# Up projection of a two-layer decoder trunk: the 512-column and the 256-column products alternate row block by row block

## The chip, the core and the metric

The kernel runs on one core of one Trainium2 chip. The metric is the device time of one execution in microseconds (us). A core has TensorE for matrix products (PE in the profile, PEld where it loads weights), VectorE (DVE), ScalarE (ACT), GpSimd (POOL) and SyncE (SP), whose queue issues the transfers between device memory and on-chip memory. Products accumulate in PSUM, in banks of 128 partitions by 512 numbers of 32 bits.

## The reference, cut to what matters

Two layers, each with a mixing part (two groups of attention heads, left out here) and a multilayer perceptron with a squared ReLU. The change lies in `h @ w_up`. There are 256 tokens, the model width is 1024 and the hidden width 4096.

```python
for l in range(DEPTH):                      # DEPTH = 2
    ...
    x = x + _rms_norm(mix, g_post_mix[l])
    h = _rms_norm(x, g_pre_mlp[l])
    y = jnp.square(jax.nn.relu(h @ w_up[l])) @ w_down[l]
    x = x + _rms_norm(y, g_post_mlp[l])
```

All data is float32.

## The kernel before

**How a float32 product is made.** TensorE works on a reduced form of float32 here (type fp32r in the profile). Each operand is split into two parts: `hi` is the rounded value, written by ScalarE (`whi`, `aT`, `xT` with ACTIVATE), and `lo` is what is left, written by VectorE (`wlo` and so on with TENSOR_TENSOR). A product a·b is then hi·hi + hi·lo + lo·hi, summed in PSUM.

**Up projection** (function `up`, from line 1388). The hidden width is cut into 8 chunks of 512 (`fc`), the first of which has a function of its own (`up0`). For each of the chunks 1 to 7, `up` goes through 4 blocks `b` of 128 hidden columns. A block has one split weight of 128 x 1024 (`hi` and `lo`, eight row blocks `k` of 128 x 128) and one PSUM bank `ps` from the tag `s` (three banks). `xT[0]` and `xT[1]` are the hi and the lo part of the transposed activations, and `xT[2]` is the view that holds both beside each other: 2 x 256 = 512 columns for each `k`. So one product of `hi[:, k]` with the 512 columns gives hi·hi in the first half of the bank and hi·lo in the second, and one product of `lo[:, k]` with the 256 columns of `xT[0]` adds lo·hi to the second half. A block has eight of the one and eight of the other, and each loads its own 128 x 128 weights. Before, the eight products of 512 columns come first (lines 1394 to 1396) and then the eight of 256 columns (lines 1397 to 1399). ScalarE then takes the second half out of the bank, VectorE adds the first half to it (lines 1405 and 1406), and for each pair of blocks ReLU, square and the split into `aT` follow (lines 1407 to 1413).

Everything of this that TensorE does appears in the profile as `s<-xT,whi` (128x512) and `s<-xT,wlo` (128x256): 2 layers x 7 chunks x 4 blocks x 8 = 448 of each.

**Down projection.** After the 64 products of a chunk's up projection come the 48 of the down projection of the chunk before it (`down`), 512 columns each, into the four banks of the tags `x` and `acc`, which are held over all chunks.

**What sets the order.** The kernel is recorded first (class `Recorder`) and then ordered by a list scheduler with costs of its own. TensorE takes the ready product that was recorded first. All products into one PSUM bank keep their recorded order. ScalarE and VectorE take what is due first, where the due times are worked back from the planned order of TensorE's products. Each engine then runs its list in order. Weights come through three rings: 9 raw tiles that SyncE's queue fills, 7 `whi` and 7 `wlo` tiles; loads are recorded 12 weights ahead and splits one ahead, and the scheduler may pull them further forward. All recorded instructions are issued at line 392, so that the profile shows that line for all of them, and they are told apart by the names of their tiles.

Of the kernel before, what the change touches and what calls it, by code (L numbers as in the profile page):

```python
# [503 lines left out]
def trunk(nc, A, consts_in, out, sbp, pp):  # L504
    def tile(shape, dtype, name, tag=None, bufs=1):
        return nc.tile(sbp[(tag or name) not in OPERANDS], shape, dtype, name, tag, bufs)

    def psum(tag):
        return nc.tile(pp, [P, 512], F32, tag, tag, {"acc": 2, "x": 2, "s": 3, "o": 1}[tag], psum=True)

    def small(shape, name, bufs=2):
        return tile(shape, F32, name=name, tag=name, bufs=bufs)
# [50 lines left out]
    def weight(*key):  # L563
        return W.get(index[key])
# [210 lines left out]
    for l in range(DEPTH):  # L775
# [612 lines left out]
        def up(fc, then=None):  # L1388
            a = [tile([P, 4, S], F32R, name="aT", tag=f"act{j}", bufs=2) for j in range(2)]
            for b in range(4):  # L1390
                hi, lo = weight(l, "up", fc, b)

                ps = psum("s")
                for k in range(8):
                    nc.tensor.matmul(ps, hi[:, k, :], xT[2][:, k].rearrange("p j n -> p (j n)"), start=k == 0, stop=False,
                                     skip_group_check=True)
                for k in range(8):
                    nc.tensor.matmul(ps[:, S:], lo[:, k, :], xT[0][:, k, :], start=False, stop=k == 7,
                                     skip_group_check=True)
                if then is not None and b == 1:  # L1400
                    then()
                if b % 2 == 0:
                    h = tokt("h")
                d = h[:, (b % 2) * S:(b % 2) * S + S]
                nc.scalar.activation(d, ps[:, S:], AF.Copy)
                nc.vector.tensor_add(d, ps[:, :S], d)
                if b % 2:
                    rl = small([P, 512], "rl")
                    nc.scalar.activation(rl, h, AF.Relu)
                    nc.vector.tensor_mul(h, rl, rl)  # L1410
                    d = [y[:, b - 1:b + 1, :].rearrange("p b n -> p (b n)") for y in a]
                    nc.scalar.activation(d[0], rl, AF.Square)
                    nc.vector.tensor_sub(d[1], h, d[0].bitcast(F32))
            return a
# [42 lines left out]
        for fc in range(8):  # L1457
            if fc < 7:
                nxt = up(fc + 1, then)
                then = None  # L1460
# [83 lines left out]
```

## Time and profile before

| | |
|---|---|
| median of 3 timed runs | 626.17 us (625.88 to 626.36) |
| profiled execution, its own time | 626.18 us |
| profiled execution, span from the first to the last instruction | 624.4 us |
| TensorE matmul busy | 615.1 us, 99% of the span |
| weight loads busy | 517.5 us, 83% |
| VectorE busy | 481.0 us, 77% |
| ScalarE busy | 378.4 us, 61% |
| read from device memory | 114.00 MB, 184 GB/s over the span |
| granted TensorE clock, mean | 0.998 of full speed |

Rows of the profile's groups read: line, engine, operation, tile written <- tiles read, shape, count | busy us, mean ns of one | idle time ahead of them. Rows of a timeline read: start in us from the span's start, length in us, engine, line, operation, and how many instructions in a row were merged. A matmul's length is more than its turn on the engine: products are pipelined, and the time that one adds is seen from its start to the start of the next.

### The profile page before, as it was taken

The numbers are of one execution on the slowest core, as the hardware profiler recorded it, in microseconds if no ns is written. First come the engines' busy times: TensorE is split into PE (matmuls) and PEld (weight loads), VectorE is DVE, ScalarE is ACT, GpSimd is POOL, SyncE is SP. The second block draws the span as 40 slices with busy tenths as digits, with TensorE's granted clock in tenths as the row PEclk, the third lists the DMA queues.
The fourth block names the chain that finished last, engine by engine and source line by source line (L and its number), as shares of the span: only waits on it lengthen the run. The fifth ranks groups of instructions, "written<-read, shape, count | busy, mean of one in ns | idle before, by whom it ended". The sixth has DMA issues, their size and how long they took to land.

```text
span 624.4 us, 9952 instructions
## 1 busy us (share of the span) xinstructions
PE 615.1 (99%) x3572; PEld 517.5 (83%) x3572; DVE 481.0 (77%) x1077; ACT 378.4 (61%) x736; POOL 0.2 (0%) x4
## 2 busy tenths in 40 slices
PE   9999999999999999999999999999999999999995
PEld 6988986788888888888888989778888888888884
DVE  6878999989986557566698899997997666566544
ACT  7757777577665455555566657764776555455432
POOL 0000000000000000000000000000000000000000
PEclk9999999999999999999999999999999999999999
DMA  8987446218766556654346883422396566556001
GB/s 322 403 341 257 150 153 199 88 56 318 266 192 203 194 175 201 198 180 136 102 156 218 303 290 118 164 81 90 105 318 204 183 186 209 180 189 193 22 1 68
DMA packets 33601, 115.70 MB, mean 185 GB/s; under 512 B 3984, under 2 KB 4112, under 8 KB 33552
## 3 DMA queue, kind: packets, MB, share of 16 engines
q1 hardware_dynamic: 33552, 115.07, 55.2%
q8 instruction: 28, 0.46, 0.3%
q14 instruction: 21, 0.17, 0.1%
HBM read 114.00 MB, written 1.05 MB: 184 GB/s over the span
## 4 chain that ended last, share of the span: by engine, by line
PE 91%; DVE 4%; DMA 2%; ACT 1%; issue 1%; DVEq 0%; SPq 0%
PE s L392 34%; PE acc L392 28%; PE x L392 24%; PE o L392 6%; DVE pr L392 2%; DMA wraw<-in_w_in_dram 1%; DVE wlo L392 1%; DMA first<-in_first_dram 1%; ACT whi L392 1%; ACT rl L392 0%; DVE cum L392 0%; DVE prT L392 0%; DVE st L392 0%; DVE prX L392 0%; ACT xT L392 0%
## 5 line engine op out<-in xcount | busy, mean ns | idle before, releaser
L392 DVE TENSOR_TENSOR wlo<-wraw,whi 128x1024 fp32r<-128x1024 f32 (+1 forms) x188 | 224.9, 1202 | 86.3 <-ACT whi L392 85.7
L392 ACT ACTIVATE whi<-wraw 128x1024 fp32r<-128x1024 f32 (+1 forms) x188 | 195.5, 1044 | 134.0 <-PE acc L392 70.3
L392 PE MATMUL s<-xT,whi 128*128 128x512 f32 x448 | 112.0, 392 | 0.0
L392 PEld LDWEIGHTS s<-xT,whi 128*128 128x128 f32 x448 | 81.4, 189 | 15.2
L392 PE MATMUL acc<-whi,aT 128*128 128x512 f32 x256 | 88.6, 390 | 0.0
L392 PE MATMUL x<-whi,aT 128*128 128x512 f32 x256 | 88.4, 390 | 0.0
L392 PEld LDWEIGHTS s<-xT,wlo 128*128 128x128 f32 x448 | 61.1, 190 | 4.4
L392 PE MATMUL s<-xT,wlo 128*128 128x256 f32 x448 | 62.5, 282 | 0.0
L392 PEld LDWEIGHTS acc<-whi,aT 128*128 128x128 f32 x256 | 48.0, 188 | 9.9
L392 PEld LDWEIGHTS x<-whi,aT 128*128 128x128 f32 x256 | 48.1, 188 | 9.6
L392 ACT ACTIVATE pr<-pr,st 128x256 f32<-128x256 f32 (+1 forms) x96 | 42.9, 450 | 15.6 <-DVE st L392 14.3
L392 PE MATMUL x<-wlo,aT 128*128 128x512 f32 x128 | 50.0, 390 | 0.0
L392 PE MATMUL acc<-wlo,aT 128*128 128x512 f32 x128 | 49.9, 390 | 0.0
L392 PE MATMUL acc<-xT,whi 128*128 128x256 f32 x256 | 48.8, 286 | 0.0
L392 PEld LDWEIGHTS acc<-xT,whi 128*128 128x128 f32 x256 | 40.4, 190 | 2.2 <-issue 1.2
L392 PE MATMUL x<-whi,xT 128*128 128x512 f32 x112 | 36.8, 400 | 0.4 <-ACT xT L392 0.3
L392 PE MATMUL acc<-xT,wlo 128*128 128x256 f32 x128 | 36.4, 285 | 0.0
L392 PE MATMUL acc<-whi,xT 128*128 128x512 f32 (+1 forms) x128 | 36.0, 352 | 0.0
L392 ACT ACTIVATE rl<-h 128x512 f32<-128x512 f32 x28 | 17.6, 629 | 18.2 <-DVE h L392 18.2
L392 PEld LDWEIGHTS acc<-wlo,aT 128*128 128x128 f32 x128 | 24.0, 188 | 5.0
L392 PEld LDWEIGHTS x<-wlo,aT 128*128 128x128 f32 x128 | 24.1, 188 | 4.5
L392 ACT ACTIVATE rl<-x 128x512 f32<-128x512 f32 x24 | 14.7, 612 | 21.6 <-PE x L392 16.6
(231 smaller groups left out, 974.7 us busy)
## 6 DMA issues: line engine op xcount, KB each, us to landing
wraw<-in_w_up_dram SPq DMA_DIRECT2D x64, 512.0 KB, 3.8
wraw<-in_w_down_dram SPq DMA_DIRECT2D x64, 512.0 KB, 3.6
wraw<-in_w_in_dram SPq DMA_DIRECT2D x36, 512.0 KB, 4.7
wraw<-in_w_out_dram SPq DMA_DIRECT2D x16, 512.0 KB, 6.2
w<-in_cmp_w_k_dram SPq DMA_DIRECT2D x8, 512.0 KB, 5.5
w<-in_cmp_w_v_dram SPq DMA_DIRECT2D x8, 512.0 KB, 5.8
first<-in_first_dram SPq DMA_DIRECT2D x7, 384.0 KB, 6.3
wraw<-in_w_in_dram SPq DMA_DIRECT2D x8, 288.0 KB, 4.2
```

The costliest lines, as they stand in the source:

```text
L392: getattr(getattr(self.nc, op.engine), name)(*[real(v) for v in args], **{k: real(v) for k, v in kw.items()})
```

## The change

The second loop header goes, so that the product of 256 columns is recorded right after the product of 512 columns of the same row block `k`. Both loops had the same range. The number of products, their operands, the first (`start`) and the last (`stop`) of each bank stay as they are; only the order within each of the 56 blocks differs.

```diff
                 for k in range(8):
                     nc.tensor.matmul(ps, hi[:, k, :], xT[2][:, k].rearrange("p j n -> p (j n)"), start=k == 0, stop=False,
                                      skip_group_check=True)
-                for k in range(8):
                     nc.tensor.matmul(ps[:, S:], lo[:, k, :], xT[0][:, k, :], start=False, stop=k == 7,
                                      skip_group_check=True)
                 if then is not None and b == 1:
```

In the program that comes out, TensorE's list has the same products in the same order outside these blocks, and within them the two kinds by turns. The lists of ScalarE and VectorE, which the scheduler orders by due times, differ in some places from the first changed block on (a split of a weight changes places with a step of the activation, above all); SyncE's list of transfers is the same.

## The prediction

> **What bounds the kernel now.** I read the page first: the busy shares, the granted clock over the span, the chain that ended last, and the groups of the changed products.
>
> ```profile
> PE 615.1 (99%) x3572; PEld 517.5 (83%) x3572; DVE 481.0 (77%) x1077; ACT 378.4 (61%) x736; POOL 0.2 (0%) x4
> ...
> PEclk9999999999999999999999999999999999999999
> ...
> PE 91%; DVE 4%; DMA 2%; ACT 1%; issue 1%; DVEq 0%; SPq 0%
> ...
> L392 PE MATMUL s<-xT,whi 128*128 128x512 f32 x448 | 112.0, 392 | 0.0
> ...
> L392 PE MATMUL s<-xT,wlo 128*128 128x256 f32 x448 | 62.5, 282 | 0.0
> ```
>
> TensorE is busy through 99% of the span at its full clock, 91% of the chain is its own work, and the two groups that the change reorders never stood idle for anything (0.0 in the last column). So a stretch of the up projection costs what its products cost on TensorE, and a change there reaches the end undiminished, to gain or to lose. Next I read the chain in order of time, for the size of an up stage, and the windows over one stage.
>
> ```profile
> 166.93 11.15 PE s L392 x64
> ...
> 584.82 11.15 PE s L392 x64
> ```
>
> ```profile
> core 0: us, PE busy (x) PEld busy (x) DVE busy (x) ACT busy (x) POOL busy (x), PEclk, DMA share, GB/s
> 144.24:155.81 11.57, 11.57 (x68) 10.14 (x67) 11.15 (x16) 7.78 (x12) 0.00 (x0) 1.00 0.87 315
> 166.77:177.92 11.15, 11.15 (x66) 9.83 (x65) 10.68 (x15) 8.03 (x15) 0.00 (x0) 1.00 0.62 195
> 451.89:463.54 11.65, 11.65 (x70) 10.32 (x69) 11.61 (x16) 8.12 (x12) 0.00 (x0) 1.00 0.93 329
> ```
>
> These are the first and the last of 12 equal stages of 64 products: 11.15 us each, though VectorE's load and the transfers differ between stages. The first up stage of each layer also holds other products (11.57 and 11.65 us, the outer rows of the windows); I price its own 64 alike. So the changed part is 14 stages of 11.15 us, 156.1 us, a quarter of the span. A stage has 32 pairs of one 512 and one 256: **348.4 ns a pair** as it is now.
>
> Then TensorE's timeline of one stage, for what each kind costs by itself, and the view by tile for the lengths.
>
> ```profile
> 166.77 1.98 PE L392 MATMUL s<-xT,whi 128*128 128x512 f32 x8
> 168.58 1.12 PE L392 MATMUL s<-xT,wlo 128*128 128x256 f32 x8
> 169.54 2.00 PE L392 MATMUL s<-xT,whi 128*128 128x512 f32 x8
> 171.38 1.12 PE L392 MATMUL s<-xT,wlo 128*128 128x256 f32 x8
> 172.33 2.00 PE L392 MATMUL s<-xT,whi 128*128 128x512 f32 x8
> 174.17 1.11 PE L392 MATMUL s<-xT,wlo 128*128 128x256 f32 x8
> 175.12 2.00 PE L392 MATMUL s<-xT,whi 128*128 128x512 f32 x8
> 176.96 1.12 PE L392 MATMUL s<-xT,wlo 128*128 128x256 f32 x8
> 177.92 0.40 PE L392 MATMUL x<-whi,aT 128*128 128x512 f32 x1
> ```
>
> ```profile
> L392 PE MATMUL s<-xT,whi x448: 389/389/478, 144.2 to 594.6; 128*128 128x512 f32 x150
> L392 PE MATMUL s<-xT,wlo x448: 277/283/283, 146.1 to 595.7; 128*128 128x256 f32 x150
> ```
>
> From start to start, eight 256s take 168.58 to 169.54, 0.96 us: 120 ns each. Eight 512s take 1.81 us (226 each) where they follow other 512s (166.77 to 168.58), but 1.84 us (230 each) where they follow 256s (169.54 to 171.38). So going back from 256s to 512s is not free: the four blocks take 2.77, 2.79, 2.79 and 2.80 us, and the three dearer ones are those that follow 256s. Lengths are modelled, but they follow the step: 389 against 226 and 283 against 120 are both 163 more, so a step is the length less 163 ns, finer than the timeline's rounding to 10 ns.
>
> **The change, part by part.** Nothing is added or removed: TensorE runs the same 448 + 448 products with as many weight loads, in 448 alternating pairs, and its list outside the blocks is the same. So the sum has one term, the price of a pair by turns, and some side effects.
>
> *The pair.* No up stage alternates, so the price comes from the nearest rows: one spot where 512s stand singly among 256s, of the same type and with their own weights, and one where two 512s stand together.
>
> ```profile
> 359.47 0.40 PE L392 MATMUL acc<-xT,whi 128*128 128x256 f32 x2
> 359.71 0.40 PE L392 MATMUL x<-kx,qS 128*128 128x512 f32 x1
> 359.94 0.28 PE L392 MATMUL acc<-xT,wlo 128*128 128x256 f32 x1
> 360.06 0.40 PE L392 MATMUL x<-kx,qS 128*128 128x512 f32 x1
> 360.30 0.40 PE L392 MATMUL acc<-xT,whi 128*128 128x256 f32 x2
> 360.54 0.28 PE L392 MATMUL acc<-xT,wlo 128*128 128x256 f32 x1
> ```
>
> ```profile
> L392 PE MATMUL x<-kx,qS 128*128 128x512 f32 x2 | 0.8, 400 | 0.0
> ...
> L392 PE MATMUL acc<-xT,wlo 128*128 128x256 f32 x1 | 0.3, 281 | 0.0
> ```
>
> ```profile
> 63.18 0.28 PE L392 MATMUL acc<-xT,wlo 128*128 128x256 f32 x1
> 63.30 0.63 PE L392 MATMUL x<-kx,qS 128*128 128x512 f32 x2
> 63.77 0.39 PE L392 MATMUL acc<-xT,whi 128*128 128x256 f32 x2
> 64.00 0.28 PE L392 MATMUL acc<-xT,wlo 128*128 128x256 f32 x1
> ```
>
> The first and second of these fences are one spot (timeline, and groups in the window 359.70 to 360.29). From the first 512's start to 360.30 is 0.59 us for 512, 256, 512; with the next 256 (half of the 0.24 to 360.54) the two pairs take 0.71 us, **355 ns a pair**. The lengths agree: 400 less 163 is 237 for a 512 and 281 less 163 is 118 for the 256 between them, together 355. So a single 512 after a 256 costs some 11 ns more than in a run, and the 256 after it gives back only 2. In the third fence the pair of 512s takes 0.47 us, 235 each, and the two 256s after it 0.23, 115 each: there the give-back is larger. Bounds for a pair by turns:
>
> - low end 346: the 512 costs 232 (a first one after 256s; 0.23 at 359.71) and the 256 gets 114, its shortest (277 less 163 in the view by tile);
> - high end 361: 241 for the 512 (0.24 at 360.06, the later of the two, when the alternation had gone on longest) and a full 120 for the 256;
> - taken 355.5, the row's own mean over two pairs, which is the only one that alternates.
>
> At 355.5 a stage takes 32 x 355.5 = 11.38 us, 0.23 more than 11.15; 14 stages give **+3.2 us**. The low end gives 11.07 and -1.1 us, the high end 11.55 and +5.6 us.
>
> *The lo weights are needed sooner.* The first `wlo` product stood 8 x 226 = 1.81 us after the block began and will stand 0.23 after it, so VectorE's split must be done 1.6 us sooner. The shortest lead is at the first block of layer 0:
>
> ```profile
> 137.91 3.49 DVE L392 TENSOR_TENSOR wlo<-wraw,whi 128x1024 fp32r<-128x1024 f32 x3
> ...
> 144.24 2.00 PE L392 MATMUL s<-xT,whi 128*128 128x512 f32 x8
> ```
>
> Counting VectorE's `wlo` writes against the blocks, this block's is the second of the three, which ends near 137.91 + 2/3 x 3.49 = 140.24, 4.0 us before the block even starts. It costs nothing while that cover stands; without it TensorE, which takes its list in order, would stop at the second product of a block, with the rest of the block and the 48 down products behind it, for as long as the split is late.
>
> *Weight tiles come free later.* The last hi product ends a block's use of `whi` some 0.84 us later (seven 256s of 120 are now ahead of it). ScalarE's next `whi` write into that tile waits that much longer, and `wlo` follows.
>
> ```profile
> ACT whi L392 <- PE s L392: 49.5, 49, 1.5
> ```
>
> From the waits: 49 such writes waited for an `s` product already. The same 4.0 us covers the 0.84 together with the 1.6. The last product of a block, after which ScalarE reads the bank and the bank is freed, is the same one as before.
>
> *ScalarE's and VectorE's lists* differ by swaps such as a `wlo` split (1.2 us) ahead of the square `h<-rl`. What these feed, `aT`, is read by the down stage after the next up stage, over 11 us later. Free of cost by that cover; SyncE's list is unchanged, so no transfer passes another in its queue.
>
> The sum, against the profiled execution's own 626.18 us (span 624.4 and 1.8 around it; the median of the runs shown is 626.17, so no correction): 626.18 + 3.2 = **629.4 us**.
>
> **The rivals.**
>
> *Order does not matter.* A pair costs 227 + 120 = 347 whatever follows what, and the 27 to 30 ns that a block after 256s pays now (2.79 and 2.80 against 2.77) go. A stage is then 32 x 347 = 11.10, 14 stages give -0.6: **625.5 us**. For it: the steady steps in both runs, and weight loads that start with the product before theirs (a PEld row stands at 359.71 too). Against it: the 237 at the mixed spot. The Trainium skill, TensorE: Matmul & The Clock Gate, sections "Back-to-back issue gap" and "LDWEIGHTS (loading the stationary operand)", states just such a rule: a step of N/2.4 + 2.5 ns for products by themselves, and a load of 128 columns in about 107 ns, which as an estimate would hide under either product. By it a pair would take about 325 ns in both orders; the trace has 227 and 120, so its step is not what runs here.
>
> ```profile
> 359.71 0.19 PEld L392 LDWEIGHTS acc<-xT,wlo 128*128 128x128 f32 x1
> ```
>
> *The long product makes room for the short one* (the other side: faster). If the disturbance needs a run of 256s to build up, the 512s keep their 227 and each 256 after a 512 takes 114: 341 a pair, 10.91 a stage, -3.4 us: **622.8 us**. For it: the 277 of the shortest `wlo` products and the 0.23 for two 256s at 63.77. Against it: at 360.06 one single 256 ahead was enough to make the next 512 dear. It decides at a pair below 345.6 ns, the price at which the time falls by 0.2%.
>
> *Every return to 512s pays in full.* A block that follows 256s costs about 0.02 to 0.03 us more now, for one return in eight pairs. If each of the pairs paid 20 ns, a pair would be 367, a stage 11.74, +8.3: **634.5 us**. Against it: at the mixed spot the 256 gave a little back, and the whole was 355.
>
> That the change does not do what it says is ruled out by the built order: 448 alternating pairs, nothing else moved on TensorE.
>
> **How the numbers follow.** My forecast, that the mixed spot's price holds (351 to 361 a pair, 627.4 to 631.8 us), gets 0.55: it rests on one row that alternates for two pairs, with other operands. Order without effect gets 0.22, the faster rival 0.16, the full price 0.07. A measurement of this kernel can tell about 0.2% from no change, 1.25 us, which is 2.8 ns a pair. Slower by more than that: 0.55 + 0.07 = 0.62; within it: 0.22; faster: 0.16. The range goes from 624.6, just under the low end of the pair's price (-1.1 us gives 625.1), to 632.0, just above its high end (631.8); it leaves out most of the faster rival and the full price, some 0.2 together.
>
> **What would show it.** In the changed kernel's timeline a stage of 64 products should take about 11.4 us instead of 11.15, the `s<-xT,whi` products should have a mean length near 400 ns instead of 392, and `s<-xT,wlo` near 281 instead of 282. The stages of the down projection and of the mixing part should keep their lengths. Mean lengths of 389 and 277 would show the faster rival, 389 and 283 the one without effect. If TensorE's idle time ahead of `s` products is no longer 0.0 and VectorE's `wlo` ends it, the cover of 4.0 us was misjudged. The prediction is wrong if what disturbs the 512s at the mixed spot comes from their own operands there (another reading pattern) and not from the 256 ahead of them.

## The result and the profile after

| | before | after |
|---|---|---|
| median of the timed runs | 626.04 us (625.86 to 626.37, 6 runs) | 628.19 us (627.87 to 628.61, 6 runs) |
| ratio to before, 95% interval | | 1.0034 [1.0021, 1.0047] |
| profiled execution, own time | 626.18 us | 628.57 us |
| span | 624.4 us | 626.8 us |
| one up stage of 64 products | 11.15 us | 11.29 us |

Slower by 2.15 us, a third of a per cent. From the page of the kernel after: the busy shares and the two changed groups.

```profile
PE 617.9 (99%) x3572; PEld 518.0 (83%) x3572; DVE 480.6 (77%) x1077; ACT 377.2 (60%) x736; POOL 0.2 (0%) x4
...
L392 PE MATMUL s<-xT,whi 128*128 128x512 f32 x448 | 158.9, 399 | 0.0
L392 PE MATMUL s<-xT,wlo 128*128 128x256 f32 x448 | 125.8, 281 | 0.0
```

The mean length of a 512 went from 392 to 399 ns, that of a 256 from 282 to 281, and there is still no idle time ahead of either. The busy column must not be read as a cost: 112.0 and 62.5 us became 158.9 and 125.8 only because pipelined products of one group overlap each other when they stand together, and then count once. From the chain in order of time, the first and the last of the 12 equal stages:

```profile
167.33 11.29 PE s L392 x64
...
587.03 11.29 PE s L392 x64
```

Each is 0.14 us longer. The first stages of the two layers grew alike (the pieces of the chain below: 5.65 + 6.09 against 5.58 + 6.03 for layer 0, 11.73 against 11.59 for layer 1).

```profile
144.70 5.65 PE s L392 x32
150.58 6.09 PE s L392 x36
...
453.24 11.73 PE s L392 x68
```

```profile
144.40 5.58 PE s L392 x32
150.22 6.03 PE s L392 x36
...
452.05 11.59 PE s L392 x68
```

(The second fence is the kernel before.) So 14 stages give 14 x 0.14 = 2.0 us of the 2.4 by which the two spans differ. Where is the rest? TensorE's timeline shows the ends of a down stage, before and after:

```profile
177.92 0.40 PE L392 MATMUL x<-whi,aT 128*128 128x512 f32 x1
...
188.82 0.62 PE L392 MATMUL s<-xT,whi 128*128 128x512 f32 x2
```

```profile
178.46 0.40 PE L392 MATMUL x<-whi,aT 128*128 128x512 f32 x1
...
189.40 0.39 PE L392 MATMUL s<-xT,whi 128*128 128x512 f32 x1
```

10.90 and 10.94 us for the same 48 products: what an up stage by turns leaves behind is worked off in the down stage, 0.04 us in each of 11 such stages, 0.4 us. (The stage behind the first up stage of each layer is 0.02 us shorter instead.) And this execution was already 0.3 us late at its first up product (144.54 against 144.24), ahead of anything that changed, because the first products of the kernel ran slower in it:

```profile
4.71 0.72 PE L392 MATMUL x<-whi,xT 128*128 128x512 f32 x2
```

```profile
4.71 1.21 PE L392 MATMUL x<-whi,xT 128*128 128x512 f32 x2
```

(First before, then after.) Between the layers the profile after gained about as much back: the chain's piece for the first stage of layer 1 stands 1.19 us later than before, where 0.3 + 7 x 0.14 + 5 x 0.04 = 1.5 had been collected. The late start is a difference between executions; whether the gain between the layers is one too, or comes from the rescheduled lists, is not shown. 2.0 + 0.4 + 0.3 - 0.3 gives the 2.4 us.

How a pair goes by turns is seen in TensorE's timeline of the kernel after:

```profile
167.51 0.40 PE L392 MATMUL s<-xT,whi 128*128 128x512 f32 x1
167.74 0.28 PE L392 MATMUL s<-xT,wlo 128*128 128x256 f32 x1
167.86 0.40 PE L392 MATMUL s<-xT,whi 128*128 128x512 f32 x1
168.10 0.28 PE L392 MATMUL s<-xT,wlo 128*128 128x256 f32 x1
168.22 0.40 PE L392 MATMUL s<-xT,whi 128*128 128x512 f32 x1
168.46 0.28 PE L392 MATMUL s<-xT,wlo 128*128 128x256 f32 x1
168.57 0.40 PE L392 MATMUL s<-xT,whi 128*128 128x512 f32 x1
```

The steps repeat every three pairs: 0.23 + 0.12, 0.24 + 0.12, 0.24 + 0.11. Three pairs take 168.57 - 167.51 = 1.06 us, 353 ns a pair, where undisturbed steps would be 227 + 120 = 347. The clock granted over these stages is 1.00 of full speed in both kernels, so a slower clock is not the reason.

### The profile page after: what moved, and what is told of

Same layout as the page of the kernel before. It is cut to its first block, busy times and chain, and to the rows that moved or that the text cites. A ratio compares the mean times of both kernels' runs of the same rounds, so it can differ in the third digit from the quotient of the medians.

```text
span 626.8 us, 9953 instructions
## 1 busy us (share of the span) xinstructions
PE 617.9 (99%) x3572; PEld 518.0 (83%) x3572; DVE 480.6 (77%) x1077; ACT 377.2 (60%) x736; POOL 0.2 (0%) x4
## 4 chain that ended last, share of the span: by engine, by line
PE 92%; DVE 4%; ACT 1%; DMA 1%; issue 1%; DVEq 0%
PE s L392 34%; PE acc L392 28%; PE x L392 24%; PE o L392 7%; DVE pr L392 2%; DMA wraw<-in_w_in_dram 1%; DVE wlo L392 1%; ACT whi L392 1%; ACT rl L392 0%; DVE cum L392 0%; DVE prT L392 0%; DVE st L392 0%; DVE prX L392 0%; DVE gz L392 0%; DVE x L392 0%
## 5 line engine op out<-in xcount | busy, mean ns | idle before, releaser
L392 PE MATMUL s<-xT,whi 128*128 128x512 f32 x448 | 158.9, 399 | 0.0
L392 PE MATMUL s<-xT,wlo 128*128 128x256 f32 x448 | 125.8, 281 | 0.0
L392 PEld LDWEIGHTS s<-xT,whi 128*128 128x128 f32 x448 | 84.2, 188 | 20.7
L392 PEld LDWEIGHTS s<-xT,wlo 128*128 128x128 f32 x448 | 84.6, 189 | 0.5
L392 PE MATMUL s<-cst,pr 128*128 128x128 f32 x144 | 27.3, 278 | 0.0
```

Of the source, the lines that this page charges most:

```text
L392: getattr(getattr(self.nc, op.engine), name)(*[real(v) for v in args], **{k: real(v) for k, v in kw.items()})
```

## The experiments

The question behind them: what makes a 512 dear when a 256 stands ahead of it, and what sets the price? All kernels differ from the kernel before only in the product loops of `up`; the lines with a minus below are those of the kernel after. Of them, only those of e3 (timed as e6) and e5 were timed over several executions; each of the others ran once. So the yardstick is the length of a stage in the chain, since the 12 equal stages of a run agree within 0.01 us; undisturbed steps would make it 32 x 346.7 = 11.09 us.

### Is it the half of the bank, or room for the weight load?

`e1_first_half` adds the short product into the other half of the bank:

```diff
-                    nc.tensor.matmul(ps[:, S:], lo[:, k, :], xT[0][:, k, :], start=False, stop=k == 7,
+                    nc.tensor.matmul(ps[:, :256], lo[:, k, :], xT[2][:, k].rearrange("p j n -> p (j n)")[:, :256], start=False, stop=k == 7,
```

> By turns as in the change, but the 256-column product adds into the first half of the bank (columns 0 to 255) in place of the second; it reads the same 256 columns, and the sum over both halves is the same. Theory LOAD (a product of 256 columns is over, after about 107 ns of streaming, just when the load of the next weights is, so the next product of 512 starts disturbed) and theory WIDTH (any return from a shorter product to one of 512 columns costs a fixed 6.7 ns) both expect the stage of the change, 11.29 us for 64 products, 353 ns a pair. Theory BANK (the 512 has just written the columns that the 256 adds to, and has to be waited for) expects the extra to shrink or go: 11.10 us, 347 a pair.

The view by tile of e1 (shortest/median/longest length, then first and last start):

```profile
L392 PE MATMUL s<-xT,whi x448: 389/398/476, 145.0 to 597.9; 128*128 128x512 f32 x150
L392 PE MATMUL s<-xT,wlo x448: 277/281/284, 145.2 to 598.2; 128*128 128x256 f32 x150
```

The medians are 398 and 281, in keeping with the change's means of 399 and 281, and the chain of e1 has the change's stage:

```profile
167.77 11.29 PE s L392 x64
```

Which half of the bank the short product writes plays no part.

`e2_short_384` has the same line with 384 in place of 256:

> By turns, but the second product of each pair has 384 columns in place of 256 (all of hi and half of lo of the activations, added into columns 0 to 383; it adds products lo x lo that the kernel otherwise leaves out). Undisturbed steps would be 227 + 173 = 400 ns a pair, 12.80 us a stage of 64. Theory LOAD: the load of the next weights now fits under the 173 ns of the second product with 53 to spare, so nothing is disturbed: 12.80 us, and the 512s have their usual length of 389 ns. Theory WIDTH: 6.7 more a pair, 406.7, 13.01 us, and the 512s are some 10 ns longer than 389.

The chain of e2, first and last of its equal stages:

```profile
169.62 13.00 PE s L392 x64
...
609.90 13.00 PE s L392 x64
```

13.00 us, 406 a pair: the 6 ns are still there although the next load has half as much room again. LOAD, as an explanation of the extra, falls. (The sum is WIDTH's, but not its parts: the median 512 of e2 is 395 ns long, 6 and not 10 above 389, and the rest sits in the 384s.) No run has products of 384 columns alone: their undisturbed 173 ns is an estimate from the straight line through 120 at 256 and 227 at 512 columns, as is the 200 for 448 below. Between the two widths the kernel before bears the line out: 29 products of 288 columns in a row take 132 ns each on average there, where the line gives 133. `e7_short_448` goes on to 448:

> By turns with a second product of 448 columns (it adds products lo x lo that the kernel otherwise leaves out). Undisturbed steps: 227 + 200 = 426.7 ns a pair, 13.65 us a stage. If any step back to a wider product pays, however near the widths are, some 6.5 ns a pair are added as at 256 and at 384: 433.2 a pair, 13.86 us. If the price follows the difference of the widths it is down to 1 or 2 ns: 428, 13.70 us.

The chain of e7, the same two rows:

```profile
169.70 13.99 PE s L392 x64
...
621.91 13.99 PE s L392 x64
```

13.99 us, 437 a pair, 10.5 above the estimated undisturbed steps: both forms of the expectation are missed, since the price neither stays nor shrinks as the widths come near. `e8_short_128` goes the other way:

> By turns with a second product of 128 columns (half of the products lo x hi are left out). Undisturbed steps: 227 + 67 = 293 ns a pair, 9.39 us a stage; with 6.7 ns per return 300 and 9.60 us. If a product cannot be shorter than the load of the next weights, and 256 columns were just at that floor (theory LOAD in its other half), the 128 takes 113 to 120 like a 256 and a pair stays near 347: 11.1 us.

TensorE's timeline of e8, a pair from start to start:

```profile
168.14 0.22 PE L392 MATMUL s<-xT,wlo 128*128 128x128 f32 x1
168.20 0.44 PE L392 MATMUL s<-xT,whi 128*128 128x512 f32 x1
168.48 0.22 PE L392 MATMUL s<-xT,wlo 128*128 128x128 f32 x1
```

A pair takes 0.34 us (168.14 to 168.48), the stage 10.83: half the columns of the short product gain only 13 ns over the change's 353. That is neither of the expected stages, 9.60 and 11.1 us, but much nearer to the second, the floor's. The short product's own step is 60 ns, but the 512 behind it then takes 280. The weight loads of the same stretch show why:

```profile
168.14 0.19 PEld L392 LDWEIGHTS s<-xT,whi 128*128 128x128 f32 x1
168.25 0.19 PEld L392 LDWEIGHTS s<-xT,wlo 128*128 128x128 f32 x1
168.48 0.19 PEld L392 LDWEIGHTS s<-xT,whi 128*128 128x128 f32 x1
```

The second load starts 0.05 us after the 512 at 168.20, while in the other runs a load starts, as a rule, within 5 ns of the product ahead of its own. In 432 of the 448 pairs of e8 it follows the load before it by 108 or 109 ns (14 of the rest begin a stage), and in no other run do two loads of an up stage stand closer than 110. So there is a floor under a short product, and the spacing of the loads sets it: a pair is 108 from load to load and 232 back. The Trainium skill (TensorE: Matmul & The Clock Gate, section "LDWEIGHTS (loading the stationary operand)") puts a load of 128 columns at about 107 ns; the trace agrees, with 108 from load to load. A 256, at 114 to 120, sits just above this floor, which is why a shorter one buys so little; but 384 and 448 are far above it and pay all the same.

### Is it the widths at all?

`e9_equal_512` takes turns between the two weights with equal widths (the line of e1 with 512), and `e10_all_256` cuts each 512 in two:

```diff
-                    nc.tensor.matmul(ps, hi[:, k, :], xT[2][:, k].rearrange("p j n -> p (j n)"), start=k == 0, stop=False,
-                                     skip_group_check=True)
+                    for j in range(2):
+                        nc.tensor.matmul(ps[:, j * S:j * S + S], hi[:, k, :], xT[j][:, k, :], start=k == 0 and j == 0, stop=False,
+                                         skip_group_check=True)
```

> By turns of the two weights with equal widths: the second product of a pair has all 512 columns too (it adds products lo x lo that the kernel otherwise leaves out). The weights, the bank and the order of the row blocks are those of the change; only the difference in width is gone. If unequal widths are the cause: 2 x 226.7 = 453.3 ns a pair, 14.51 us a stage, every 512 at its usual length of 389 ns. If it is taking turns between the two weight tiles on one bank that disturbs the stream, the extra of 6 to 11 ns a pair that 256, 384 and 448 columns had stays: 460 to 464, 14.7 to 14.9 us.

> By turns with equal widths from the other side: each product of 512 columns is cut into two of 256 with the same weights, which are loaded twice. Three products of 256 a row block. If unequal widths are the cause, each takes its 120 ns, 360 a row block, 11.52 us a stage of 96 products, and no step differs from 120 inside a stage; a fixed disturbance of any change of weights, width apart, gives 367 and 11.73.

The view by tile and the chain, first of e9 and then of e10:

```profile
L392 PE MATMUL s<-xT,whi x448: 389/389/481, 144.2 to 641.5; 128*128 128x512 f32 x150
L392 PE MATMUL s<-xT,wlo x448: 389/389/398, 144.4 to 641.8; 128*128 128x512 f32 x150
```

```profile
170.27 14.51 PE s L392 x64
...
627.63 14.51 PE s L392 x64
```

```profile
L392 PE MATMUL s<-xT,whi x896: 277/283/365, 144.2 to 601.3; 128*128 128x256 f32 x180
L392 PE MATMUL s<-xT,wlo x448: 283/283/288, 144.4 to 601.4; 128*128 128x256 f32 x150
```

```profile
167.23 11.51 PE s L392 x96
...
590.18 11.51 PE s L392 x96
```

14.51 / 32 = 453 a pair is 2 x 226.7, and 11.51 / 96 = 120 a product: no extra in either. (The shortest 256s of e10, 277, are the first of a stage, behind the 512s of the down projection.) Taking turns between weights on one bank costs nothing here. **The extra belongs to neighbours of unequal width.** Neither kernel is an improvement: 672.41 and 631.89 us against 625.82, since both add work to TensorE.

### What sets the price: the length of the runs

`e3_two_and_two` and `e4_four_and_four` group the products of each block by 2 and by 4: so many of 512 columns, then as many of 256 (shown for 2; the lines left out are the two products as they were):

```diff
+                for g in range(0, 8, 2):
+                    for k in range(g, g + 2):
...
+                    for k in range(g, g + 2):
...
```

> Two products of 512, then two of 256, by turns: half as many returns to 512s as in the change. A fixed price of 6.7 ns per return (theory WIDTH) gives 347 + 3.3 = 350.3 a pair, 11.21 us a stage. Theory WORK-OFF (a return sets up a debt that the following 512s pay off over five of them, and that a change to 256s gives back in part: the fewer 512s follow, the less is paid) goes by the one place of the kernel before where two 512s stand together, 234 + 236 + 115 + 113 for two pairs: 349 a pair, 11.17 us.

> Four products of 512, then four of 256, by turns. Theory WIDTH: 6.7 ns per return over four pairs, 348.7 a pair, 11.16 us a stage, less than two and two. Theory WORK-OFF: the first four 512s pay 6, 9, 1 and 6 ns as after the 256s of the kernel before and little of it comes back: 351 a pair, 11.24 us, more than two and two and more than eight and eight (11.15).

The chains of e3 and of e4:

```profile
167.27 11.14 PE s L392 x64
...
584.92 11.14 PE s L392 x64
```

```profile
166.90 11.20 PE s L392 x64
...
585.61 11.20 PE s L392 x64
```

The order is WORK-OFF's (two and two below eight and eight, four and four above it), each some 0.03 to 0.04 us cheaper than it said. WIDTH's fixed price put them the other way round and falls. WORK-OFF is a description drawn from steps of the kernel before; what inside TensorE would be owed, no run shows. `e5_sixteen` carries it to 16, over two blocks in two banks (left out are the loops over the eight row blocks, as they were):

```diff
+                if b % 2 == 0:
+                    ws = [weight(l, "up", fc, b + i) for i in range(2)]
+                    banks = [psum("s") for _ in range(2)]
+                    for ps, (hi, lo) in zip(banks, ws):
...
+                    for ps, (hi, lo) in zip(banks, ws):
...
+                ps = banks[b % 2]
```

> Two blocks at once, in two of the three banks: sixteen products of 512, then sixteen of 256. Half as many returns to 512s as in the kernel before. If the debt of a return is paid in full within five 512s, as theory WORK-OFF has it, a return costs the same 20 ns after a run of 16 as after one of 8: a stage of 64 has two groups, the first of which comes from the down projection's 512s and has none to pay, so 2 x 5546.7 - 7 + 20 = 11.107 us against 11.146, 14 stages 0.55 us less: about 625.5 us where the kernel before takes 626.0. If instead the debt grows with the run of 256s behind it, a return costs some 40 ns and the time stays that of the kernel before (11.13 to 11.15). If a bank is held too long and TensorE has to wait for one, it is slower by the waits (a second bank is needed about 1.8 us after the 512s of a pair of blocks begin).

TensorE's timeline of e5, one up stage:

```profile
188.73 3.79 PE L392 MATMUL s<-xT,whi 128*128 128x512 f32 x16
192.35 2.08 PE L392 MATMUL s<-xT,wlo 128*128 128x256 f32 x16
194.27 3.82 PE L392 MATMUL s<-xT,whi 128*128 128x512 f32 x16
197.92 2.08 PE L392 MATMUL s<-xT,wlo 128*128 128x256 f32 x16
199.83 0.40 PE L392 MATMUL x<-whi,aT 128*128 128x512 f32 x1
```

The sixteen 512s after the down projection take 3.62 us, those after 256s 3.65: 0.03 for one return, as after a run of eight (1.84 against 1.81). Behind the 96 products of 256 of an e10 stage, too, the next five 512s take 28 ns more than five undisturbed ones, as many as behind eight. So the debt does not grow with the run of 256s, and the stage is 11.10 us by these rows (188.73 to 199.83), 11.11 in the chain. Its time: 625.39 us against 626.16 of the kernel before on the same chip, ratio 0.9988 [0.9979, 0.9997]. The sign is that of its 14 x 0.04 = 0.6 us, but a gain of a tenth of a per cent is hardly more than can be told.

> The kernel of e3 again, timed. Its profile gave 14 stages of 11.137 us (9 ns less than before each) and down stages 17 ns shorter each, some 0.3 us in all: theory WORK-OFF and the profile expect 625.7 us where the kernel before takes 626.0, which is less than a measurement can tell from no change; theory WIDTH (a fixed price per return, +0.9 us) expects 627.

625.45 us, ratio 0.9992 [0.9983, 1.0001]: not told apart from no change, and the 627 of WIDTH lies above its slowest run (626.82).

By run length, the stage as the starts in the trace give it, to the nanosecond, and what it has above 11.093 us:

| 512s, then 256s | stage, us | above undisturbed steps, us | returns inside a stage |
|---|---|---|---|
| 1 and 1 (the change) | 11.290 | 0.197 | 31 |
| 2 and 2 | 11.137 | 0.044 | 15 |
| 4 and 4 | 11.200 | 0.107 | 7 |
| 8 and 8 (before) | 11.146 | 0.053 | 3 |
| 16 and 16 | 11.106 | 0.013 | 1 |

The first 256s of a stage, behind 512s that had nothing to pay, give back some 7 ns together (113 and 119 in place of 120 each); without this a return costs about 7 ns, 3, 16, 20 and 20. One and one is the worst not because its returns are dear but because it has 31 of them. That they cost 7 and those of two and two only 3 is not explained by WORK-OFF, by which fewer 512s behind a return pay less.

## Why the prediction was right, and where it was off

**What bounds.** Right: a stage costs what TensorE's products cost, and the difference reached the end undiminished: 2.0 us from the up stages and 0.4 from the down stages behind them stand against 2.4 between the two profiled executions, and against 2.15 between the medians, whose runs spread over 0.5 and 0.7 us.

**The price of a pair.** The mechanism and the sign were right and the size was 2.7 ns too large: 355.5 taken, 352.8 measured (11.29 / 32), so 0.14 us a stage in place of 0.23, and 628.2 us in place of 629.4. The mixed spot of the kernel before shows two pairs, of 0.35 and 0.36 us, and its mean was taken for the pattern's; the change repeats three, of 0.35, 0.36 and 0.35 us, so that the dear one counts for a third and not for half. To the nanosecond, the trace has 233 + 117 and 241 + 120 at the spot, and 232 + 118, 240 + 120 and 236 + 114 in the change: the spot is the cycle without its third pair. The bounds were wider than the cycle allows: 346 would need its cheapest 512 and its cheapest 256 in one pair, where they never stand together, and 361 the dear pair every time.

**A term that was missing.** The down stage behind an up stage by turns is 0.04 us longer, 0.4 us in all. The prediction had said that the other stages keep their lengths. Together, 14 x 0.14 + 11 x 0.04 = 2.4 us stand against the 3.2 of the sum. That the total came out nearer than the price of a pair is luck: the missing term has the opposite sign of the error in the price.

**The spot's own operands.** The prediction named as its weak point that the spot's reading pattern, and not the 256 ahead, might make its 512s dear. The change itself has the spot's steps with the operands of the up projection, and e9 and e10 show that with these the extra comes and goes with the widths alone.

**The lo weights, the weight tiles, the lists.** Right, no cost. The waits of TensorE after the change hold no `wlo`:

```profile
PE o L392 <- DVE warm L392: 1.2, 1, 1.2
PE x L392 <- ACT oT L392: 0.4, 1, 0.4
PE x L392 <- ACT xT L392: 0.3, 1, 0.3
PE s L392 <- DVE kW L392: 0.2, 1, 0.2
PE x L392 <- DVE oT L392: 0.2, 1, 0.2
```

The later release of `whi` shows on ScalarE alone, and TensorE's waits show nothing of it:

```profile
ACT whi L392 <- PE s L392: 60.9, 51, 1.6
```

60.9 us of waiting for `s` products where 49.5 stood, 1.2 us a wait in place of 1.0: 0.2 more, much less than the 0.84 that the prediction put on each.

**The rivals.** Order without effect (625.5) is refuted by the 353 a pair. The rule of the Trainium skill (TensorE: Matmul & The Clock Gate, section "Back-to-back issue gap") for products by themselves has a step depend on its own width alone; in this stream of loads and products that is so only among equal widths, and with 227 and 120 ns, not its 216 and 109. The long product that makes room for the short one (622.8) is refuted too, though its evidence was real: a 256 of 114 occurs in each cycle, but the 512s around it pay more than it gives. The full price at every return (634.5) is refuted: about 7 ns in place of 20.

**What stays open** is what inside TensorE is out of step after a change of width. The runs show its outside: it is paid off over a few 512s where a run is long enough, it repeats alike in every stage, whatever the transfers and the other engines do there, it depends neither on the bank's half nor on taking turns between weights, and 448 columns beside 512 pay more (10.5 ns a pair, by the estimated step) than 256 do (6). Neither WIDTH nor WORK-OFF accounts for all of this.

## What to carry to other kernels

Where TensorE is the bound, do not alternate products of two widths one by one: with weights of their own, products of 256 or of 512 columns followed their like at 120 and 227 ns also where they took turns between weights, and each return to the wider product cost 3 to 20 ns that no idle column shows. Longer runs are not always better: two and two was as cheap here as eight and eight, and four and four dearer than either. All of it is small, 0.18 us of an 11.1 us stage between the best order and the worst. Look for it in the mean length of a group and in the start-to-start steps, since the busy share stays at 99%. When the nearest row for a new pattern covers only a few products, ask whether it shows a whole cycle before taking its mean as the price.

## What the runs showed of the hardware that was not expected

- Products of unequal width side by side: 353 ns a pair of 512 and 256 where the steps of equal ones add up to 347; 406 against an estimated 400 with 384; 437 against an estimated 427 with 448; nothing extra with 512 and 512 or 256 and 256.
- The price per return is not even in order of the run length: about 7 ns at runs of 1, 3 at 2, 16 at 4, 20 at 8 and at 16.
- A product of 128 columns between 512s saves only 13 ns over one of 256 (340 against 353 a pair): it takes 60 ns itself and the 512 behind it 280, because two weight loads never stand closer than 108 ns in these stages.
